# A two-layer hybrid trunk on one core: the layer passage reordered, one power of two a layer for the mix, and one product of the output norm as a square on ScalarE

## The chip, the cores and the metric

The kernel runs on one core of a Trainium2 chip. The metric is the device time of one execution in microseconds (us), lower is better. Before the change the median of three runs is 1673.27 us (1671.96 to 1673.34).

## The reference

Two layers, each with one pre-norm mixer. `h = rmsnorm(x) * g` goes through one input projection, whose columns feed three head groups: a gated short convolution, stick-breaking attention, and gated linear attention (GLA). Each branch is multiplied by a gate of its own, the three are concatenated and go through one output projection into the residual stream.

```python
D_MODEL, SEQ, DEPTH = 2048, 512, 2
def _layer(x, norm_g, w_in, ..., w_out):
    h = _rmsnorm(x, norm_g)
    proj = h @ w_in                                  # 2048 x 7184
    cv_h, cv_b, cv_c, cv_g, sb_q, sb_k, sb_v, sb_g, gl_q, gl_k, gl_v, gl_g, gl_lr = split(proj)
    y_conv = short_conv(cv_h, cv_b, cv_c, ...) * silu(cv_g)
    y_sb = stick_breaking(rmsnorm(sb_q), rmsnorm(sb_k), sb_v) * silu(sb_g)
    g = log_sigmoid(gl_lr @ gla_w_up + gla_b_up) / 16
    y_gla = rmsnorm(gla(gl_q, gl_k, gl_v, g), gla_on_g) * silu(gl_g)
    mix = concat([y_conv, y_sb, y_gla])
    return x + mix @ w_out
```

All of it is float32. Several of the gains drawn for the test are large, so the kernel scales operands by powers of two before it splits them.

## The kernel before

**Three-pass products.** TensorE (PE) multiplies float16. Each float32 operand is scaled by a power of two and split into a high and a low float16 part; a product is high*high + high*low + low*high. So every weight and every activation needs one pass on ScalarE (ACT) for the high part and one on VectorE (DVE) for the low part.

**Weight groups.** The weights stream from DRAM in groups of 256 columns, in a fixed list (`specs`): for GLA V, V with the low-rank columns, Q, K and two gate groups; then the convolution and the attention groups; then eight output groups, `gi` 0 to 7. A group passes through these steps, each for two halves of the rows: `fetch` (L332, a 1 MB DMA from SP's queue into an `st` buffer), `wmax` (L344, a sum of squares on ACT into `wm`), an all-reduce on GpSimd (POOL, L357, `wgm`), `wscale` (L360, L369, L371 on DVE: `wq`, `ws`, `wu`), and then four pieces `w` with the high part on ACT (L419) and the low part on DVE (L423). `st` buffers are reused: a fetch waits on SP until the low part of an earlier group has read its buffer.

**Order.** The code is written in program order and a scheduler orders each engine's instructions by a simulated timeline; `tc.high_priority()` lifts a piece. Engines work in order. So small edits of the code can move instructions on several engines.

**PSUM.** `cols(o)` multiplies one group into two PSUM banks of the pool `psp` (three banks), one per half of the 256 columns. The banks are free for the next group once they have been read for the last time. In GLA, q and k (`qT`, `kT`) are read twice from PSUM: the largest magnitude (L921 on DVE), then, after an all-reduce on POOL (L185, `qTgm`, `kTgm`) and `pow2` (L191 to L193, three small operations on DVE), the scaled copy (L930 on ACT). Behind K come the two gate groups, evicted by L816 to L823 (`gx` in the waits). GLA's source and target tiles (`th`) are zeroed by POOL (L907), as are the tiles `zw` and `raw` for column sums of x (L972).

**Mix.** The outputs of the branches get one common power of two. Each of eight pieces has a bound; `mixscale` turns each into a power of two by `pow2` and writes it to one column of `pmix`. `mix_unit` (L1079) all-reduces `pmix` on POOL, takes the largest and derives the factor.

**Output norm of GLA** (L1061 to L1075, eight times). The mean square `ms` is made by PE, `r` = exp(-0.5 ln(ms + eps)) on ACT, and one Newton step on DVE: (ms + eps) * r (L1070), * r (L1071), - 3, * r (L1072), * -0.5 * o (L1073).

**Layer passage.** Group `gi` 7 of layer 0 is multiplied block by block of 128 tokens, t = 0 to 3. `finish` adds the residual (L1359 on DVE, into the tile `x`, called `xt` in the code), stores it to DRAM (`xs<-x`, L1341, SP) and sums its squares (L1347, ACT). `xprep` then prepares the next layer's input for that block: `xnorm` (small operations, L490 to L494 on DVE, L198 and L199 on ACT), `xgain` (L499, two halves, in place in `x`), and the split. For t = 0 and 1 the split is made first (L536 ACT, L537 DVE, tiles `th` for the two halves of t = 0, `raw` and `qp` for those of t = 1) and each part is transposed by a DMA on SP's queue (L539). For t = 2 and 3 PE transposes (L509) into PSUM (`psz`, two banks), ACT takes the high part (L511) and DVE the low (L518), which frees the bank. The results are the tiles `act_183` (high) and `act_184` (low), from which the next layer's first group is multiplied (L649).

Of the kernel before, what the change touches and what calls it, by code (L numbers as in the profile page):

```python
# [10 lines left out]
AF = mybir.ActivationFunctionType  # L11
# [6 lines left out]
P = 128  # L18
# [21 lines left out]
def hybrid_trunk(ctx, tc, x, norm_g, w_in, conv_w, conv_b, sb_qn_g, sb_kn_g,  # L40
# [274 lines left out]
        with tc.high_priority():  # L315
            load_(i)

    staged, peak, scales = {}, {}, {}

    def junk(n):  # L320

# [18 lines left out]
    def wmax(i, h):  # L340

        if h == 0:
            peak[i] = sm(2 + len(specs[i][2]) // 2, "wm")
        S.activation(junk(HK * GW).rearrange("p (k n) -> p k n", k=HK), staged[i][h], AF.Square,  # L344
                     accum_out=peak[i][:, h:h + 1])
# [135 lines left out]

    ssq = sm(NT * NG, "ssq").rearrange("p (t g) -> p t g", g=NG)
    xscale = {}

    def xnorm(l, t):

# [9 lines left out]

    def xgain(t, h):
        xv = xt[t // 2][:, t % 2, h * (D // 2):(h + 1) * (D // 2)]
        V.scalar_tensor_tensor(xv, xv, xscale[t], gb[h], ALU.mult, ALU.mult)  # L499

    xps = {}

# [285 lines left out]
    for l in range(depth):  # L788
# [39 lines left out]

        pmix = sm(8, "pmix")

        def mixscale(j, m, tag):

            pow2(pmix[:, j:j + 1], m, -12.0, tag)

        def spill(k, y):

            nc.sync.dma_start(mixd[k], y)
# [78 lines left out]
        for tag in ("qT", "kT"):  # L916
            o = wk([P, 2, seq], tag)
            ps, u = cols(o)
            mx = sm(2, tag + "mx")
            for c in range(2):  # L920
                V.tensor_reduce(mx[:, c:c + 1], ps[c], AX.X, ALU.max, apply_absolute_value=True)  # L921
            gm = allmax(mx, 2, tag)
            m = sm(1, tag + "m")
            V.tensor_tensor(m, gm[:, 0:1], gm[:, 1:2], ALU.max)
            p2 = sm(1, tag + "p2")
            pow2(p2, m, -14.0, tag)
            s_ = sm(1, tag + "s")
            V.reciprocal(s_, p2)
            for c in range(2):
                S.activation(o[:, c, :], ps[c], AF.Copy, scale=s_)  # L930
# [9 lines left out]
        for p in range(2):  # L940
            gmx = sm(1, "ggm")
            gg.append(gate(gmx))
            m = sm(1, "gb")
            V.tensor_tensor(m, gmx, onmax[:, l:l + 1], ALU.mult)
            mixscale(6 + p, m, "g")

        def split_src(e, dst, b):

# [20 lines left out]
        for p in range(2):  # L969
# [88 lines left out]
            for hh in range(2):  # L1058
                ops_ = ops2[:, hh, :]

                o_ = wk([P, seq], "za")  # L1061
                S.activation(o_, ops_, AF.Copy, scale=gu[:, p:p + 1])
                sq = wk([P, seq], "e")
                S.activation(sq, o_, AF.Square)
                ms = bank(psm, "m")
                T.matmul(ms, avg.to_broadcast([P, P]), sq, start=True, stop=True)
                r_ = wk([P, seq], "e")
                S.activation(r_, ms, AF.Ln, bias=epst)
                S.activation(r_, r_, AF.Exp, scale=-0.5)
                V.scalar_tensor_tensor(sq, ms, EPS, r_, ALU.add, ALU.mult)  # L1070
                V.tensor_tensor(sq, sq, r_, ALU.mult)  # L1071
                V.scalar_tensor_tensor(r_, sq, 3.0, r_, ALU.subtract, ALU.mult)  # L1072
                V.scalar_tensor_tensor(r_, r_, -0.5, o_, ALU.mult, ALU.mult)  # L1073
                V.scalar_tensor_tensor(o_, r_, pcol("on", l), gg[p][:, hh, :], ALU.mult, ALU.mult)
                spill(12 + 2 * p + hh, o_)  # L1075

        def mix_unit():

            pmx = allmax(pmix, 8, "r")  # L1079
            V.tensor_reduce(pmx[:, 0:1], pmx, AX.X, ALU.max)  # L1080
            ratio[l] = sm(1, "rub")
            V.tensor_scalar(ratio[l], pmx[:, 0:1].bitcast(I32), 1.0, (51 - 127 - MAGIC) * 2.0 ** 23, ALU.mult, ALU.add)
            rp = sm(1, "rpm")
            V.reciprocal(rp, pmx[:, 0:1])
            return rp
# [62 lines left out]
        def conv_out(j, y, then=lambda: None):  # L1148

            g = gate()  # L1150
            V.tensor_tensor(y, y, g, ALU.mult)
            bound = sm(2, "cm")

            def limit(m):
                V.tensor_reduce(m, y, AX.XY, ALU.max, apply_absolute_value=True)
                return m

            then()
            s_ = None
            if j:  # L1160
                V.tensor_scalar(bound[:, 1:2], limit(bound[:, 0:1]), loaded[cursor[0]][1], 2.0 ** 28, ALU.mult, ALU.mult)
                mixscale(j, bound[:, 1:2], "c")
                s_ = mix_unit()
            ps, u = cols(None if j else wk([P, 2, seq], "qT"))
            for c in range(2):
                V.scalar_tensor_tensor(m32[0][:, 2 + c, :] if j else y[:, c, :], ps[c], u, y[:, c, :], ALU.mult, ALU.mult)
            if not j:
                mixscale(j, limit(bound[:, 0:1]), "c")
                for c in range(2):
                    spill(2 * j + c, y[:, c, :])  # L1170
            return s_
# [94 lines left out]
        for j in range(4):  # L1266
# [40 lines left out]
            if j:  # L1307
                vh, vl, vu = value_group()
            g = gate(bm[:, 1:2])
            m = sm(1, "sbm")  # L1310
            V.tensor_scalar(m, bm[:, 1:2], vu, 2.0 ** 28, ALU.mult, ALU.mult)
            mixscale(2 + j, m, "b")
            attend(j, *qkT, vh, vl, vu, g)
            go()

# [22 lines left out]
        def land(gi, dst, t, n, c0, w, ot):  # L1338

            to = out[0] if last else xs  # L1340
            nc.sync.dma_start(to[t * P:(t + n) * P, c0:c0 + w].rearrange("(t p) c -> p t c", p=P), dst)  # L1341
            if not last:
                if ot is not None:
                    nc.sync.dma_start(xt[t // 2][:, t % 2:t % 2 + n, c0:c0 + w], dst)

        def square(gi, t, dst):
# [107 lines left out]
```

## Time and profile before

| | |
|---|---|
| Median of three runs | 1673.27 us |
| The profiled execution | 1674.31 us, of it a span of 1672.2 us |
| TensorE clock granted | 0.998 |
| PE busy | 1640.1 us of 17450 matmuls, 98% |
| DVE busy | 1420.5 us, 85% |
| ACT busy | 1233.2 us, 74% |
| POOL busy | 74.0 us, 4% |

"Busy" counts instructions that do work; an engine's waits are its idle time. PE is nearly always busy, so a change can save at most the waits of PE, unless it changes the products themselves, which this one does not.

### The profile page before, as it was taken

To read this page: it belongs to the slowest core of one execution; us is meant where nothing else is said; L and a number is where in the kernel's file an instruction comes from. 1 tells how busy PE (TensorE), PEld (TensorE's weight loads), DVE (VectorE), ACT (ScalarE), POOL (GpSimd) and SP (SyncE) were. 2 spreads that over 40 slices of the span, in tenths; PEclk is the share of its full clock that TensorE was granted. 3 is DMA by queue.
4 is the path that set the end of the run, shared out by engine and by line. 5 is a ranking of instruction groups with operands and counts; after the bars stand their busy time and mean duration, and the time that the engine had idled before them with its cause. 6 is when DMAs were issued, how large, how long until landed. Compare 5 with 4: busy or idle time off the path is not lost.

```text
span 1672.2 us, 40635 instructions
## 1 busy us (share of the span) xinstructions
PE 1640.1 (98%) x17450; PEld 1331.6 (80%) x17450; DVE 1420.5 (85%) x2368; ACT 1233.2 (74%) x1695; POOL 74.0 (4%) x96
## 2 busy tenths in 40 slices
PE   7999999999999999999999999999999999999999
PEld 5744748999999985799976447589989998858999
DVE  7967898899898987888778588988989899979896
ACT  8767776697878787667766678776969696976663
POOL 0010000000000000000000100000000000000000
PEclk9999999999999999999999999999999999999999
DMA  7393332436363649245765624324464546473441
GB/s 259 104 206 94 102 107 68 130 85 169 101 161 112 159 126 259 78 158 161 226 140 143 159 76 121 107 82 109 118 155 118 155 116 158 123 237 102 153 153 52
DMA packets 308099, 227.58 MB, mean 136 GB/s; under 512 B 127650, under 2 KB 301004, under 8 KB 307408
## 3 DMA queue, kind: packets, MB, share of 16 engines
q1 hardware_dynamic: 298912, 215.55, 46.4%
q10 hardware_dynamic: 9008, 9.45, 1.8%
q8 instruction: 136, 2.23, 0.6%
q14 instruction: 43, 0.35, 0.1%
HBM read 179.88 MB, written 14.68 MB: 116 GB/s over the span
## 4 chain that ended last, share of the span: by engine, by line
issue 30%; PE 13%; DVE 5%; ACT 4%; DMA 2%; POOL 1%; SPq 0%; POOLq 0%; DVEq 0%; ACTq 0%
PE psp L676 3%; PE psp L649 2%; PE psp L673 2%; PE psp L623 2%; PE psp L622 2%; PE psp L621 2%; POOL wgm L357 1%; DVE w L437 1%; ACT w L436 1%; ACT junk L344 1%; DMA st<-in_w_in_dram 1%; DVE w L423 1%; PE psp L639 0%; PE psp L638 0%; PE psp L637 0%
## 5 line engine op out<-in xcount | busy, mean ns | idle before, releaser
L436 ACT ACTIVATE w<-st,ws 128x1024 f16<-128x1024 f32 x273 | 305.2, 1141 | 137.7 <-DVE st L441 63.7
L437 DVE SCALAR_TENSOR_TENSOR w<-st,ws,w 128x1024 f16<-128x1024 f32 x273 | 344.5, 1279 | 61.3 <-ACT w L436 58.4
L344 ACT ACTIVATE junk<-st 128x2048 uint8<-128x2048 f32 x150 | 284.9, 1899 | 22.3 <-DMA st<-in_w_in_dram 16.0
L673 PEld LDWEIGHTS <-w 128*128 128x128 f16 x2352 | 230.2, 98 | 32.2 <-DVE u L716 2.3
L637 PE MATMUL psp<-w,act 128*128 128x256 f16 x896 | 244.1, 273 | 0.0
L638 PE MATMUL psp<-w,act 128*128 128x256 f16 x896 | 244.1, 273 | 0.0
L639 PE MATMUL psp<-w,act 128*128 128x256 f16 x896 | 243.9, 273 | 0.0
L676 PE MATMUL psp<-w,act 128*128 128x128 f16 x3600 | 214.7, 219 | 5.9 <-DVE raw L727 2.5
L621 PE MATMUL psp<-act,w 128*128 128x512 f16 x576 | 218.3, 379 | 2.0 <-DVE gx L823 1.3
L622 PE MATMUL psp<-act,w 128*128 128x512 f16 x576 | 218.3, 379 | 0.0
L623 PE MATMUL psp<-act,w 128*128 128x512 f16 x576 | 218.1, 379 | 0.0
L676 PEld LDWEIGHTS <-act 128*128 128x128 f16 x3600 | 205.0, 98 | 9.6 <-issue 5.1
L423 DVE SCALAR_TENSOR_TENSOR w<-st,ws,w 128x1024 f16<-128x1024 f32 x148 | 187.9, 1278 | 28.5 <-ACT w L419 28.1
L419 ACT ACTIVATE w<-st,ws 128x1024 f16<-128x1024 f32 x144 | 161.9, 1140 | 32.5 <-PE psp L623 22.5
L676 PE MATMUL psp<-w,s 128*128 128x128 f16 x2688 | 156.3, 219 | 0.5 <-DVE vv L719 0.5
L673 PE MATMUL psp<-s,w 128*128 128x256 f16 x1344 | 156.6, 274 | 0.0
L676 PEld LDWEIGHTS <-s 128*128 128x128 f16 x2688 | 152.1, 98 | 2.1 <-issue 1.9
L357 POOL PARTITION_ALL_REDUCE wgm<-wm x75 | 57.8, 770 | 1444.3 <-ACT junk L344 1343.2
L673 PE MATMUL psp<-act,w 128*128 128x256 f16 x1008 | 118.3, 273 | 0.0
L649 PE MATMUL psp<-w,act 128*128 128x256 f16 (+1 forms) x960 | 111.7, 277 | 6.0 <-DMA act<-raw 2.6
L649 PEld LDWEIGHTS <-act 128*128 128x128 f16 x960 | 93.8, 99 | 22.0 <-issue 2.9
L622 PEld LDWEIGHTS <-w 128*128 128x128 f16 x576 | 56.3, 98 | 67.6 <-issue 2.5
(361 smaller groups left out, 2652.4 us busy)
## 6 DMA issues: line engine op xcount, KB each, us to landing
st<-in_w_in_dram SPq DMA_DIRECT2D x120, 1024.0 KB, 5.8
st<-in_w_out_dram SPq DMA_DIRECT2D x32, 1024.0 KB, 5.7
m<-mixd SPq DMA_DIRECT2D x24, 256.0 KB, 5.4
x<-in_x_dram SPq DMA_DIRECT2D x4, 1024.0 KB, 11.9
qT<-in_x_dram ACTq DMA_DIRECT2D x8, 512.0 KB
qT<-xs ACTq DMA_DIRECT2D x8, 512.0 KB, 3.8
out_dram<-kT SPq DMA_DIRECT2D x16, 256.0 KB, 2.1
mixd<-e SPq DMA_DIRECT2D x12, 256.0 KB
```

Of the source, the lines that this page charges most:

```text
L344: S.activation(junk(HK * GW).rearrange("p (k n) -> p k n", k=HK), staged[i][h], AF.Square, accum_out=peak[i][:, h:h + 1])
L436: his.setdefault(i, []).append(S.activation(hi, x, AF.Copy, scale=scales[i]))
L437: V.scalar_tensor_tensor(lo, x, scales[i], hi, ALU.mult, ALU.subtract)
L621: T.matmul(o, wh, xh[:, k, :, :], start=st_, stop=False)
L622: T.matmul(o, wh, xl[:, k, :, :], start=False, stop=False)
L623: T.matmul(o, wl, xh[:, k, :, :], start=False, stop=en)
L637: T.matmul(o, xh[:, k, t, :], wh, start=k == 0 and t % 2 == 0, stop=False, skip_group_check=True)
L638: T.matmul(o, xh[:, k, t, :], wl, start=False, stop=False, skip_group_check=True)
L639: T.matmul(o, xl[:, k, t, :], wh, start=False, stop=k == lastk, skip_group_check=True)
L649: T.matmul(o[:, :n], a_[:, k, t, :], wview(w, part, k, n), start=i == 0 and k == 0, stop=i == 2 and k == KT - 1)
L673: T.matmul(o[:, :2 * P], ww, x[xi][:, k, :, :], start=first, stop=final, skip_group_check=True)
L676: T.matmul(o[:, t * P:(t + 1) * P], x[xi][:, k, t, :], ww, start=first, stop=final, skip_group_check=True)
```

## The change

1. **Mix.** `mixscale` is gone: the raw bounds go into `pmix`, and one `pow2` is applied to their maximum in `mix_unit`.
2. **Output norm.** The two DVE products (ms + eps) * r * r become a square of r on ACT and one DVE product with it.
3. **GLA q and k.** Both banks are copied to SBUF on ACT at once (the new L923); the maximum and the scaled copy (now L926 and L935) read and write that copy.
4. **Passage.** The result of `gi` 7 goes to a tile `ot` (tag `kT`) of its own, kept in `tail`, and is stored from there; `xgain`'s second half is made in two pieces, 768 columns in place and 256 columns from `ot`. The squares of the second half of `gi` 6 (t = 2 and 3) are issued behind the squares of the next weight group (`issue_after`).

```diff
-        S.activation(junk(HK * GW)..., staged[i][h], AF.Square, accum_out=peak[i][:, h:h + 1])
+        squares[i] = S.activation(junk(HK * GW)..., staged[i][h], AF.Square, accum_out=peak[i][:, h:h + 1])
...
     def xgain(t, h):
         xv = xt[t // 2][:, t % 2, h * (D // 2):(h + 1) * (D // 2)]
-        V.scalar_tensor_tensor(xv, xv, xscale[t], gb[h], ALU.mult, ALU.mult)
+        n = D // 2 - (GW if h and tail else 0)
+        V.scalar_tensor_tensor(xv[:, :n], xv[:, :n], xscale[t], gb[h][:, :n], ALU.mult, ALU.mult)
+        if h and tail:
+            V.scalar_tensor_tensor(xv[:, n:], tail[0][:, t, :], xscale[t], gb[h][:, n:], ALU.mult, ALU.mult)
...
-        def mixscale(j, m, tag):
-            pow2(pmix[:, j:j + 1], m, -12.0, tag)
...
             for c in range(2):
+                if ps[c].tensor is not o.tensor:
+                    with tc.high_priority():
+                        S.activation(o[:, c, :], ps[c], AF.Copy)
+            ps = [o[:, c, :] for c in range(2)]
+            for c in range(2):
                 V.tensor_reduce(mx[:, c:c + 1], ps[c], AX.X, ALU.max, apply_absolute_value=True)
...
-            m = sm(1, "gb")
-            V.tensor_tensor(m, gmx, onmax[:, l:l + 1], ALU.mult)
-            mixscale(6 + p, m, "g")
+            V.tensor_tensor(pmix[:, 6 + p:7 + p], gmx, onmax[:, l:l + 1], ALU.mult)
...
-                V.scalar_tensor_tensor(sq, ms, EPS, r_, ALU.add, ALU.mult)
-                V.tensor_tensor(sq, sq, r_, ALU.mult)
+                S.activation(sq, r_, AF.Square)
+                V.scalar_tensor_tensor(sq, ms, EPS, sq, ALU.add, ALU.mult)
...
             V.tensor_reduce(pmx[:, 0:1], pmx, AX.X, ALU.max)
+            pow2(pmx[:, 0:1], pmx[:, 0:1], -12.0, "r")
...
-                if ot is not None:
+                if ot is not None and gi < 2:
                     nc.sync.dma_start(xt[t // 2][:, t % 2:t % 2 + n, c0:c0 + w], dst)
...
-            ot = wk([P, NT, GW], "kT") if last or gi < 2 else None
+            ot = wk([P, NT, GW], "kT") if last or gi < 2 or gi == NG - 1 else None
+            if gi == NG - 1:
+                tail.append(ot)
...
+                        if gi == NG - 2 and r:
+                            late = dst
+                            continue
...
                 for t, o, u in project_by_token(GW):
+                    if not (last or t):
+                        with tc.issue_after(squares[cursor[0]].ins):
+                            for i in range(2):
+                                square(gi - 1, 2 + i, late[:, i, :])
```

(The convolution's and the attention's calls of `mixscale` are replaced in the same way.)

The scheduler moves instructions in three places that matter below. Lines behind L344 are one to four higher after the change, so L423 stays L423 while L499 becomes L501 and L503, L537 becomes L541, and L1359 becomes L1360.

The first place is the passage. On DVE, before, the rows from the residual of t = 0 (`psp_12016`) to the first `xgain`; `w_12004` and `w_12007` are the first low parts of the next weight group:

```order
L1359 SCALAR_TENSOR_TENSOR x_9456<-psp_12016,wu_11605,qT_11983 128x256
L360 TENSOR_SCALAR wq_11996<-wgm_11997 128x1
L490 TENSOR_REDUCE xtot_12069<-ssq_9458 128x1
L369 TENSOR_SCALAR ws_12000<-wq_11996 128x1
L371 TENSOR_SCALAR wu_12002<-wq_11996,xub 128x1
L201 TENSOR_SCALAR xrm_12075<-xtot_12069 128x1
L850 TENSOR_SCALAR gu_12359<-wu_12002 128x1
L423 SCALAR_TENSOR_TENSOR w_12004<-st_11590,ws_12000,w_12004 128x1024
L1359 SCALAR_TENSOR_TENSOR x_9456<-psp_12095,wu_11605,qT_11983 128x256
L423 SCALAR_TENSOR_TENSOR w_12007<-st_11590,ws_12000,w_12007 128x1024
```

After, on the same engine, the same stretch (`w_11971` and `w_11974` are those low parts now):

```order
L360 TENSOR_SCALAR wq_11963<-wgm_11964 128x1
L369 TENSOR_SCALAR ws_11967<-wq_11963 128x1
L371 TENSOR_SCALAR wu_11969<-wq_11963,xub 128x1
L850 TENSOR_SCALAR gu_12334<-wu_11969 128x1
L423 SCALAR_TENSOR_TENSOR w_11971<-st_11560,ws_11967,w_11971 128x1024
L423 SCALAR_TENSOR_TENSOR w_11974<-st_11560,ws_11967,w_11974 128x1024
L1360 SCALAR_TENSOR_TENSOR kT_11951<-psp_11983,wu_11575,qT_11949 128x256
```

The scale of the next group and two of its low parts now stand ahead of the residual of t = 0. Further on, around the fourth residual (`psp_12265`, after the change `psp_12239`), DVE's order is, before and then after:

```order
L1359 SCALAR_TENSOR_TENSOR x_9457<-psp_12265,wu_11605,qT_11983 128x256
L423 SCALAR_TENSOR_TENSOR w_12013<-st_11592,ws_12000,w_12013 128x1024
L537 TENSOR_TENSOR raw_12163<-x_9456,raw_12163 128x1024
L204 TENSOR_TENSOR xrt_12235<-xrt_12235,xrm_12233 128x1
L537 TENSOR_TENSOR qp_12169<-x_9456,qp_12169 128x1024
```

```order
L541 TENSOR_TENSOR raw_12135<-x_9426,raw_12135 128x1024
L204 TENSOR_TENSOR xrt_12208<-xrt_12208,xrm_12206 128x1
L423 SCALAR_TENSOR_TENSOR w_11977<-st_11562,ws_11967,w_11977 128x1024
L1360 SCALAR_TENSOR_TENSOR kT_11951<-psp_12239,wu_11575,qT_11949 128x256
L205 SCALAR_TENSOR_TENSOR xrstd_12202<-xrt_12208,xr_1205_12203 128x1
L541 TENSOR_TENSOR qp_12142<-x_9426,qp_12142 128x1024
```

The low part of `raw` no longer stands behind two weight parts. At the end of the passage, before, one low part of t = 2 (L518) stands ahead of `xgain` of t = 3; after, both (L522) stand behind it and behind four weight pieces:

```order
L518 TENSOR_TENSOR act_184<-psz_12242,act_183 128x8x128
L857 TENSOR_SCALAR gu_12359<-wu_12378 128x1
L499 SCALAR_TENSOR_TENSOR x_9457<-x_9457,xrs_12330,g_9459 128x1024
L499 SCALAR_TENSOR_TENSOR x_9457<-x_9457,xrs_12330,g_9460 128x1024
L425 SCALAR_TENSOR_TENSOR w_12380<-ga_11989,ws_12376,w_12380 128x4x16
```

```order
L503 SCALAR_TENSOR_TENSOR x_9427<-kT_11951,xrs_12304,g_9430 128x256
L857 TENSOR_SCALAR gu_12334<-wu_12353 128x1
L425 SCALAR_TENSOR_TENSOR w_12355<-ga_11956,ws_12351,w_12355 128x4x16
L423 SCALAR_TENSOR_TENSOR w_12355<-st_11952,ws_12351,w_12355 128x4x256
L425 SCALAR_TENSOR_TENSOR w_12360<-ga_11956,ws_12351,w_12360 128x4x16
L423 SCALAR_TENSOR_TENSOR w_12360<-st_11952,ws_12351,w_12360 128x4x256
L522 TENSOR_TENSOR act_184<-psz_12215,act_183 128x8x128
L522 TENSOR_TENSOR act_184<-psz_12228,act_183 128x8x128
```

So the banks of t = 2 are freed later in the row than before. On SP's queue the transposes of t = 1 stand after the change as

```order
L543 DMA_TRANSPOSE act_183<-raw_12135 128x8x128
L543 DMA_TRANSPOSE act_184<-raw_12135 128x8x128
L543 DMA_TRANSPOSE act_183<-qp_12142 128x8x128
L1342 DMA xs<-kT_11951 128x256
L543 DMA_TRANSPOSE act_184<-qp_12142 128x8x128
L332 DMA st_12337<-in_w_in_dram 128x8x256
```

where before a weight fetch and a store stood between the second transpose (`qp`, high) and the third (`raw`, low); the fetch now stands behind all of them.

The second place is GLA's k in layer 1, on ACT. Before, the copies of `kT` stand behind the two squares of a weight group:

```order
L344 ACTIVATE junk_13408,wm_13407<-st_13252 128x2048
L344 ACTIVATE junk_13410,wm_13407<-st_13254 128x2048
L930 ACTIVATE kT_13101<-psp_13131,kTs_13241 128x512
L930 ACTIVATE kT_13101<-psp_13132,kTs_13241 128x512
L950 ACTIVATE th_12946<-e_13554 128x4x64
```

After, the banks are read ahead of them:

```order
L923 ACTIVATE kT_13078<-psp_13108 128x512
L419 ACTIVATE w_13248<-st_13079,ws_13244 128x1024
L923 ACTIVATE kT_13078<-psp_13109 128x512
L419 ACTIVATE w_13251<-st_13079,ws_13244 128x1024
L344 ACTIVATE junk_13382,wm_13381<-st_13231 128x2048
L344 ACTIVATE junk_13384,wm_13381<-st_13233 128x2048
L935 ACTIVATE kT_13078<-kT_13078,kTs_13220 128x512 x2
```

The third place is POOL in layer 0, before and after:

```order
L185 ISA qTgm_1165<-qTmx_1162 128x2
L972 MEMSET zw_1631 128x1024
L357 ISA wgm_1341<-wm_1335 128x2
L972 MEMSET raw_1978 128x1024
L185 ISA kTgm_1311<-kTmx_1308 128x2
```

```order
L975 MEMSET zw_1625 128x1024
L185 ISA qTgm_1167<-qTmx_1162 128x2
L357 ISA wgm_1345<-wm_1339 128x2
L975 MEMSET raw_1972 128x1024
L185 ISA kTgm_1315<-kTmx_1310 128x2
```

The zeroing of `zw` moved ahead of the all-reduce for q's maximum.

More of the change, by code (lines that the diff above doesn't have):

```diff
@@ L316, in load @@
             load_(i)
-    staged, peak, scales = {}, {}, {}
+    staged, peak, scales, squares = {}, {}, {}, {}
     def junk(n):
@@ L343, in wmax @@
             peak[i] = sm(2 + len(specs[i][2]) // 2, "wm")
-        S.activation(junk(HK * GW).rearrange("p (k n) -> p k n", k=HK), staged[i][h], AF.Square,
-                     accum_out=peak[i][:, h:h + 1])
+        squares[i] = S.activation(junk(HK * GW).rearrange("p (k n) -> p k n", k=HK), staged[i][h], AF.Square,
+                                  accum_out=peak[i][:, h:h + 1])
         if h and len(specs[i][2]) > 1:
@@ L483, in hybrid_trunk @@
     xscale = {}
+    tail = []
     def xnorm(l, t):
@@ L1151, in conv_out @@
             V.tensor_tensor(y, y, g, ALU.mult)
-            bound = sm(2, "cm")
+            bound = sm(1, "cm")
             def limit(m):
@@ L1160, in conv_out @@
             if j:
-                V.tensor_scalar(bound[:, 1:2], limit(bound[:, 0:1]), loaded[cursor[0]][1], 2.0 ** 28, ALU.mult, ALU.mult)
-                mixscale(j, bound[:, 1:2], "c")
+                V.tensor_scalar(pmix[:, j:j + 1], limit(bound), loaded[cursor[0]][1], 2.0 ** 28, ALU.mult, ALU.mult)
                 s_ = mix_unit()
@@ L1167, in conv_out @@
             if not j:
-                mixscale(j, limit(bound[:, 0:1]), "c")
+                limit(pmix[:, j:j + 1])
                 for c in range(2):
@@ L1309, in hybrid_trunk @@
             g = gate(bm[:, 1:2])
-            m = sm(1, "sbm")
-            V.tensor_scalar(m, bm[:, 1:2], vu, 2.0 ** 28, ALU.mult, ALU.mult)
-            mixscale(2 + j, m, "b")
+            V.tensor_scalar(pmix[:, 2 + j:3 + j], bm[:, 1:2], vu, 2.0 ** 28, ALU.mult, ALU.mult)
             attend(j, *qkT, vh, vl, vu, g)
```

## The prediction

> **What bounds the kernel now.** I read the page first. Its first rows give the share of each engine:
>
> ```profile
> span 1672.2 us, 40635 instructions
> PE 1640.1 (98%) x17450; PEld 1331.6 (80%) x17450; DVE 1420.5 (85%) x2368; ACT 1233.2 (74%) x1695; POOL 74.0 (4%) x96
> ```
>
> PE is idle for 1672.2 - 1640.1 = 32.1 us. The products stay as they are, so the whole gain must come out of these 32.1 us, and what DVE or ACT save elsewhere is worth nothing unless PE waits for it. The waits of PE by releaser (sum in us, times, longest) say where such places are; the first word pair is the waiting line, the second what it waited for:
>
> ```profile
> PE psp L676 <- DVE w L437: 3.5, 4, 1.1
> PE psp L649 <- DMA act<-raw: 2.6, 1, 2.6
> PE psp L676 <- DVE raw L727: 2.5, 3, 0.9
> PE psp L621 <- DVE gx L823: 1.3, 1, 1.3
> PE psp L649 <- DMA act<-th: 0.9, 2, 0.6
> PE psp L621 <- ACT kT L930: 0.7, 1, 0.7
> ```
>
> Three of the edits touch such rows. The two of L649 are the layer passage: 2.6 + 0.9 = 3.5 us. The two of L621 are GLA's banks: 0.7 us in layer 0, 1.3 us in layer 1. Together 5.5 us of 1672, 0.33%, is what the change can take away directly. PE's timeline shows the passage (start, duration, form, idle time before it in brackets):
>
> ```profile
> 849.88 1.93 PE L649 MATMUL psp<-w,act 128*128 128x256 f16 x16 [0.63 <-DMA act<-th]
> 852.11 5.71 PE L649 MATMUL psp<-w,act 128*128 128x256 f16 x48 [0.30 <-DMA act<-th]
> 857.66 2.06 PE L509 MATMUL psz<-ident,x 128*128 128x128 f32 x16
> 862.32 4.54 PE L649 MATMUL psp<-w,act 128*128 128x256 f16 x40 [2.60 <-DMA act<-raw]
> 866.70 1.04 PE L509 MATMUL psz<-ident,x 128*128 128x128 f32 x8
> ```
>
> PE waits twice for block t = 0 and once, the longest, for the low part of t = 1.
>
> **The passage, part 4.** What makes t = 0 late is the row of DVE, and ahead of that of ACT:
>
> ```profile
> 831.52 0.42 ACT L1347 ACTIVATE junk<-x 128x256 uint8<-128x256 f32 x1 [3.74 <-DVE x L1401]
> 832.65 1.91 ACT L344 ACTIVATE junk<-st 128x2048 uint8<-128x2048 f32 x1
> ```
>
> ```profile
> 834.88 0.48 DVE L1359 SCALAR_TENSOR_TENSOR x<-psp,wu,qT 128x256 f32<-128x256 f32 x1 [3.45 <-PE psp L649]
> 837.23 0.21 DVE L360 TENSOR_SCALAR wq<-wgm 128x1 f32<-128x1 int32 x1 [1.86 <-POOL wgm L357]
> 840.11 0.48 DVE L1359 SCALAR_TENSOR_TENSOR x<-psp,wu,qT 128x256 f32<-128x256 f32 x1
> 840.51 1.28 DVE L423 SCALAR_TENSOR_TENSOR w<-st,ws,w 128x1024 f16<-128x1024 f32 x1
> 842.61 2.48 DVE L499 SCALAR_TENSOR_TENSOR x<-x,xrs,g 128x1024 f32<-128x1024 f32 x2
> ```
>
> ACT idles 3.74 us for a residual of gi 6 (L1401), squares it (two squares, 831.52 to 832.65) and only then comes to the weight squares. Put behind them, the squares of gi 6 give the weight scale up to 3.74 + 1.13 = 4.9 us back; I take 4.2, as the load of ACT just before may take some. The scale (837.23) comes at 833.0, and two low parts of 1.28 us are done by about 836.8, ahead of the second residual. The residual of t = 0, which now stands behind them, goes from 834.88 to 836.8; its norm has until 840.6, so that costs nothing. `xgain` of t = 0 can start when the second residual ends, 840.11 + 0.48 = 840.6 instead of 842.61: 2.0 us earlier. Its third piece costs about 0.2 us (256 columns as in the residual's 0.48, less the 0.32 that the shortened piece saves). So the transposes of t = 0 come 1.8 us earlier, and the waits of 0.63 and 0.30 go. For t = 1:
>
> ```profile
> 853.32 1.22 DVE L537 TENSOR_TENSOR raw<-x,raw 128x1024 f16<-128x1024 f32 x1
> 859.79 1.23 DVE L518 TENSOR_TENSOR act<-psz,act 128x1024 f16<-128x1024 f32 x1
> 861.00 2.47 DVE L499 SCALAR_TENSOR_TENSOR x<-x,xrs,g 128x1024 f32<-128x1024 f32 x2
> 863.58 1.28 DVE L423 SCALAR_TENSOR_TENSOR w<-st,ws,w 128x1024 f16<-128x1024 f32 x1
> ```
>
> ```profile
> 854.81 0.53 SPq L332 DMA_DIRECT2D st<-in_w_in_dram  x1
> 856.14 2.20 SPq L539 DMA_TRANSPOSE act<-raw  x1
> ```
>
> The low part of `raw` (853.32) loses two weight parts and a residual ahead of it (2 x 1.28 + 0.48 = 3.0) and follows an `xgain` that starts about 0.7 us earlier (the residual of t = 2, which PE sets, holds it): about 849.6. On SP's queue its transpose no longer stands behind a 1 MB fetch (854.81). It was issued at 856.14 and released PE at 862.32, 6.2 us later. Of the transposes of `qp` the DMA table says (us from issue to landing, last):
>
> ```profile
> act<-qp SPq DMA_TRANSPOSE x2, 3.2
> ```
>
> Issued at about 851 it lands between 854.2 and 857.2 by these two rows; without a fetch ahead I take 3.2. PE comes to it at about 856 (857.66, less the 0.93 of waits gone, and six of these products now stand ahead of the transposes of t = 2), so this wait, 2.60, goes too, or up to 1.2 of it stays.
>
> The Trainium skill says in "DMA: Bandwidth & Descriptors", section "Queues, rings and completion order", that each of the 16 DMA engines takes a queue's descriptors in ring order; by that rule the transpose behind the fetch pays for most of its megabyte, and moving the fetch takes the wait away, the sum as above. If instead a transpose took 6.2 us by itself, 1.2 us would stay. The 6.2 us behind a fetch against 3.2 agrees with the rule, though the two were not issued at the same load.
>
> What is late next are the low parts of t = 2. Before, one is made at 859.79, ahead of `xgain` of t = 3. Now both stand behind that `xgain` (2.5 us) and two weight parts with their small companions (3.0 us), and PE's first transposes of t = 3 need the bank that they free, at 866.70 - 3.5 = 863.2 if the other waits are gone. With `xgain` of t = 3 starting at 858.5, which follows from moving the row by the 2.5 us that DVE is ahead, the first low part ends at 858.5 + 2.5 + 3.0 + 1.2 = 865.2: a wait of 2.0. If it starts 2 us earlier, none. I take 1.2 of new wait. Passage: 3.5 - 1.2 = 2.3 gained, ends 1.0 and 3.5.
>
> The fetch's other side: `st` for the second half of a later group is now issued behind the last transposes, about 3 us later than 854.81. What hides it is the stock of weights ahead of PE, which was busy without a gap from 870 to 960 (window, length, busy time of PE, PEld, DVE, ACT, POOL, clock, DMA share, GB/s):
>
> ```profile
> 870.00:960.00 90.00, 90.00 (x548) 53.26 (x547) 57.99 (x102) 54.94 (x73) 10.75 (x10) 1.00 0.60 144
> ```
>
> So I cost it at nothing; if that cover were gone it would cost up to these 3 us.
>
> **GLA q and k, part 3.** Layer 1, first ACT, then POOL, then PE:
>
> ```profile
> 949.30 1.91 ACT L344 ACTIVATE junk<-st 128x2048 uint8<-128x2048 f32 x1 [3.66 <-DMA st<-in_w_in_dram]
> 951.20 1.25 ACT L930 ACTIVATE kT<-psp,kTs 128x512 f32<-128x512 f32 x2
> 959.80 1.73 ACT L959 ACTIVATE th<-e 64x256 f16<-64x256 f32 x4 [6.03 <-POOL th L907]
> 965.33 0.67 ACT L816 ACTIVATE ga<-psp,nu 128x512 f32<-128x512 f32 x1
> ```
>
> ```profile
> 957.97 1.80 POOL L907 MEMSET th<- 128x2048 f16 x1 [4.57 <-issue]
> ```
>
> ```profile
> 969.74 0.38 PE L621 MATMUL psp<-act,w 128*128 128x512 f16 x1 [1.29 <-DVE gx L823]
> ```
>
> The gate's bank is read at 965.33 because ACT had waited for a fetch (3.66) and then for a memset (6.03). With k's banks read before, and the fetch taken out from behind transposes, ACT is 3 to 4 us earlier there, against a wait of 1.29: gained 1.2, ends 0 and 1.29. The eight new copies, 0.63 us each by L930's 1.25 for two (5.0 us), lie beside PE's products of the same groups; ACT is busy for 74%. In layer 0 the wait of 0.68 goes, but POOL's order changes:
>
> ```profile
> 93.40 0.40 POOL L185 PARTITION_ALL_REDUCE qTgm<-qTmx  x1 [6.48 <-DVE qTmx L921]
> 99.68 0.95 POOL L972 MEMSET zw<- 128x1024 f32 x1 [5.88 <-DMA s<-zw]
> ```
>
> The memset waits for a DMA until 99.68, and the all-reduce of q now waits behind it: 100.6 instead of 93.4, 7.2 us. Behind it on ACT stand q's scaled copies and GLA's decays, so its chain runs some 5 us later, and the gate banks with it. No row of layer 0 prices that. The nearest is layer 1, whose POOL has this order already: a wait of 1.29. Between 0 and 1.29 I take 0.5. Layer 0: -0.68 + 0.5 = -0.2, ends -0.7 and +0.6.
>
> **The small operations, parts 1 and 2.** Their prices (count, min/median/max ns, first and last start):
>
> ```profile
> L193 DVE TENSOR_SCALAR pmix<-bpc x8: 141/144/155, 366.8 to 1446.7; 128x1 f32<-128x1 f32 x8
> L1071 DVE TENSOR_TENSOR e<-e,e x8: 682/689/693, 209.8 to 1131.2; 128x512 f32<-128x512 f32 x8
> L1064 ACT ACTIVATE e<-za x8: 613/627/630, 203.4 to 1120.2; 128x512 f32<-128x512 f32 x8
> ```
>
> Sixteen times three operations become two times three: 42 x 0.145 = 6.1 us less on DVE. In the chain to the common factor nothing is saved: three operations that stood ahead of the all-reduce stand behind it. Eight products leave DVE, 5.5 us, and eight squares come to ACT, 5.0 us. Where PE waits for DVE (w L437 3.5, raw L727 2.5) the rows are mostly of attention and of output groups, where little of this is. I take 0.3 us of gain; ends 1.0 of gain (a sixth of those 6 us) and 0.5 of loss, should ACT's extra 10.0 us delay high parts of weights.
>
> **Sum.** 2.3 + 1.2 + 0.2 + 0.3 = 4.0 us off the profiled execution's 1674.31, which gives 1670.3. That execution lies 1.0 us over the median of the runs; against the median, 1673.27 - 4.0 = 1669.3.
>
> **Rivals.**
> *The passage gives it back* (0.30). The low parts of t = 2 keep PE for the full 2.0 us, and 1.2 of the low part of t = 1 stays: 3.5 - 3.2 = 0.3 of the passage, total 0.3 + 1.7 = 2.0, 1671.3. For it speaks DVE's busy time in the stretch; against it that the weight parts may have slid forward too.
> *Layer 0 eats it* (0.10). The late chain of q costs 1.29 at two gate banks, 2.6 in all, and layer 1 keeps its 1.29: 4.0 - 2.1 - 1.2 = 0.7, 1672.6. Against it: k's and q's banks are free early.
> *The order of the weights becomes the wait* (0.08, the other side). The residual of t = 0 stands behind two low parts, and these behind the scale. Had the scale no gain (837.23), that residual came at 841.8, and, with some 3 us for its norm (square, root, small operations), `xgain` at 845.3: 2.7 us later than 842.61, and with it all that follows; the total is 2.7 - 1.7 = +1.0, 1674.3. It is slower by more than 0.2%, 1676.6, from a scale at 839.6 on. Against it: ACT idles 3.74 us there, and the fetch of that group had long been issued:
>
> ```profile
> 818.92 2.77 SPq L332 DMA_DIRECT2D st<-in_w_in_dram  x2
> ```
>
> *The parts with no PE wait behind them* are no rival: they give nothing either way.
>
> **Numbers.** The forecast's own case has 0.52, from 1667.0 to 1670.5. All terms at their good ends give 3.5 + 1.3 + 0.7 + 1.0 = 6.5, 1666.8; the first two rivals reach to 1672.6, the third beyond. So the range is 1666.6 to 1672.8. A difference of 0.2%, 3.35 us, is about what can be told from no change: the bounds are 1669.9 and 1676.6. Of the forecast's case some four fifths lie below 1669.9 (0.42), and of the first rival a quarter, where its 2.0 us of wait shrinks (0.07): faster 0.49. Of the third rival some six tenths lie above 1676.6: slower 0.05. The remaining 0.46 is no change.
>
> **What would show it.** Right: no idle time of PE at `act<-th` and `act<-raw`, the first weight scale of the passage near 833, `xgain` of t = 0 near 840.6; no wait for kT in layer 0 or for `gx` in layer 1. Right on the rest: a new wait of PE's t = 3 transposes for L522 of 0 to 2 us. Wrong: a wait for that of over 2 us, `act<-raw` still late although no fetch stands ahead of it, waits for gate banks in layer 0 from 120 to 145 of over 1.3, or new waits in attention, where I expect none.

## The result, and the profile after

The changed kernel takes 1669.68 us (median of 12 runs, 1666.79 to 1671.14) against 1672.78 us before (12 runs, 1670.39 to 1675.82). The ratio is 0.9983, 95% interval 0.9975 to 0.9990: 3.1 us or 0.17% less, where the prediction had 4.0 us. That is a change of less than 0.2%, though the interval leaves out a ratio of 1. The page of the profiled execution:

```profile
span 1668.4 us, 40601 instructions
PE 1641.0 (98%) x17450; PEld 1332.4 (80%) x17450; DVE 1413.9 (85%) x2322; ACT 1242.0 (74%) x1711; POOL 72.8 (4%) x96
```

DVE has 6.6 us less work, ACT 8.8 more, and PE's idle time fell from 32.1 to 27.4 us. The waits of PE (sum, times, longest):

```profile
PE psp L653 <- ACT act L515: 1.6, 2, 1.4
PE psp L653 <- DMA act<-raw: 1.4, 1, 1.4
PE psp L625 <- DVE gx L827: 0.9, 1, 0.9
```

The rows of `act<-th` and of `kT` are gone, as forecast. `act<-raw` is not, `act L515` is new, and the row of `gx` belongs to layer 0 now. PE in the passage, in order of time:

```profile
835.76 14.79 PE L653 MATMUL psp<-w,act 128*128 128x256 f16 x134
851.97 6.51 PE L653 MATMUL psp<-w,act 128*128 128x256 f16 x58 [1.42 <-DMA act<-raw]
858.31 1.91 PE L513 MATMUL psz<-ident,x 128*128 128x128 f32 x16
860.06 3.00 PE L653 MATMUL psp<-w,act 128*128 128x256 f16 x26
864.42 1.95 PE L653 MATMUL psp<-w,act 128*128 128x256 f16 x16 [1.35 <-ACT act L515]
866.21 1.04 PE L513 MATMUL psz<-ident,x 128*128 128x128 f32 x8
```

Two waits, 2.8 us, stand where three stood, 3.5 us. DVE, then ACT, then SP's queue in the same stretch:

```profile
832.43 0.21 DVE L360 TENSOR_SCALAR wq<-wgm 128x1 f32<-128x1 int32 x1 [1.00 <-POOL wgm L357]
836.51 0.47 DVE L1360 SCALAR_TENSOR_TENSOR kT<-psp,wu,qT 128x256 f32<-128x256 f32 x1
839.43 2.20 DVE L501 SCALAR_TENSOR_TENSOR x<-x,xrs,g 128x1024 f32<-128x1024 f32 x2
848.19 1.22 DVE L541 TENSOR_TENSOR raw<-x,raw 128x1024 f16<-128x1024 f32 x1
864.39 2.35 DVE L522 TENSOR_TENSOR act<-psz,act 128x1024 f16<-128x1024 f32 x2
```

```profile
846.85 1.06 ACT L540 ACTIVATE raw<-x 128x1024 f16<-128x1024 f32 x1 [0.66 <-DVE x L501]
861.47 1.89 ACT L344 ACTIVATE junk<-st 128x2048 uint8<-128x2048 f32 x1
863.36 1.91 ACT L515 ACTIVATE act<-psz 128x1024 f16<-128x1024 f32 x2
```

```profile
841.82 6.17 SPq L543 DMA_TRANSPOSE act<-th  x4
848.71 2.62 SPq L543 DMA_TRANSPOSE act<-raw  x2
```

The scale of the next weight group comes at 832.43 instead of 837.23 and `xgain` of t = 0 at 839.43 instead of 842.61, so the parts of t = 0 land in time. PE stops at 850.55, for the high part of `raw`, the first of t = 1. That part was made by 847.9, its transpose was issued at 848.71 behind four of t = 0, and PE goes on with it at 851.97. PE was not through with t = 0 when it stopped. Its own order, in the built program, has changed, which the section on the change did not say: before, all 48 products of t = 0 stand ahead of the first product of t = 1; after, only 12 do, then come eight with the high part of `raw`, and the other 36 of t = 0 stand behind these. The low parts of t = 0 landed at 848.67 and 849.85 (the landings in the trace), ahead of the stop. The second wait is for the high parts of t = 2, which stand on ACT behind a weight square (861.47).

**Stage by stage.** The same product (the n-th matmul of a line; inside a stage the order can differ, so only the ends are used) can be found in two profiles. The difference of its start is PE's lead (negative: ahead of the profile before), and how the lead changes between the ends of a stage is what the stage gained or lost. The table has this for all the kernels run, in us; times are those of the profile before.

| kernel | GLA banks, layer 0 (113-229) | norm, layer 0 (229-303) | 534-767 | passage (842-900) | gates, layer 1 (900-1058) | norm, layer 1 (1058-1132) |
|---|---|---|---|---|---|---|
| the changed one | +0.13 | +0.43 | -0.39 | -1.36 | -1.53 | +0.42 |
| p_only | -0.53 | -0.01 | -2.27 | -1.23 | -1.14 | -0.03 |
| q_only | -0.40 | 0.00 | -2.74 | +1.02 | -1.34 | -0.02 |
| m_only | -0.63 | -0.02 | -1.89 | -0.04 | -0.46 | -0.03 |
| n_only | -0.38 | +0.38 | -2.50 | +0.10 | -0.52 | +0.37 |
| no_n | -0.36 | 0.00 | -2.01 | -1.49 | -1.54 | -0.02 |
| a_hi | +0.44 | +0.40 | -0.19 | -2.17 | -1.47 | +0.42 |
| b_v1 | -0.42 | +0.02 | -3.79 | -0.11 | -0.54 | -0.01 |
| best_v1 | -0.19 | 0.00 | -3.45 | -2.15 | -1.10 | -0.02 |
| a_pool | -0.92 | +0.40 | -2.40 | -1.02 | -1.54 | +0.42 |
| best2 | -0.93 | +0.01 | -3.50 | -2.11 | -1.25 | -0.04 |

A stage that an edit doesn't touch shows the scatter between executions: nothing in the norm stages (0.05), 0.4 to 0.5 in the GLA stage of layer 0 (p_only, n_only, b_v1), 0.5 in the gates (n_only, b_v1), and 2 in the stretch from 534 to 767, of which the last section tells. All leads are against one profile of the kernel before, which was slow in these stages.

### The profile page after: what moved, and what is told of

Same layout as the page of the kernel before. It is cut to its first block, busy times and chain, and to the rows that moved or that the text cites. A ratio compares the mean times of both kernels' runs of the same rounds, so it can differ in the third digit from the quotient of the medians.

```text
span 1668.4 us, 40601 instructions
## 1 busy us (share of the span) xinstructions
PE 1641.0 (98%) x17450; PEld 1332.4 (80%) x17450; DVE 1413.9 (85%) x2322; ACT 1242.0 (74%) x1711; POOL 72.8 (4%) x96
## 4 chain that ended last, share of the span: by engine, by line
PE 25%; DVE 11%; issue 10%; ACT 6%; DMA 2%; POOL 1%; SPq 1%; ACTq 0%; POOLq 0%; DVEq 0%
PE psp L680 5%; PE psp L677 5%; PE psp L653 3%; DVE w L437 3%; ACT w L436 2%; PE psp L627 2%; PE psp L625 2%; PE psp L626 2%; PE psp L642 1%; PE psp L643 1%; PE psp L641 1%; ACT junk L344 1%; DMA st<-in_w_in_dram 1%; DVE th L963 1%; DVE w L423 1%
## 5 line engine op out<-in xcount | busy, mean ns | idle before, releaser
L344 ACT ACTIVATE junk<-st 128x2048 uint8<-128x2048 f32 x150 | 284.9, 1899 | 14.8 <-DMA st<-in_w_out_dram 6.8
L677 PEld LDWEIGHTS <-w 128*128 128x128 f16 x2352 | 230.2, 98 | 32.1 <-DVE u L720 2.1
L423 DVE SCALAR_TENSOR_TENSOR w<-st,ws,w 128x1024 f16<-128x1024 f32 x148 | 187.5, 1279 | 26.5 <-ACT w L419 26.1
```

What stands on the lines that cost most here:

```text
L344: squares[i] = S.activation(junk(HK * GW).rearrange("p (k n) -> p k n", k=HK), staged[i][h], AF.Square, accum_out=peak[i][:, h:h + 1])
L677: T.matmul(o[:, :2 * P], ww, x[xi][:, k, :, :], start=first, stop=final, skip_group_check=True)
```

## The experiments

**The parts alone.** Each is the kernel before with one part of the diff. p_only is part 4 (`squares`, `tail`, `xgain` in pieces, `issue_after`), q_only part 3, m_only part 1, n_only part 2. Their core lines:

```diff
p_only  +            ot = wk([P, NT, GW], "kT") if last or gi < 2 or gi == NG - 1 else None
p_only  +                        with tc.issue_after(squares[cursor[0]].ins):
q_only  +                        S.activation(o[:, c, :], ps[c], AF.Copy)
m_only  +            pow2(pmx[:, 0:1], pmx[:, 0:1], -12.0, "r")
n_only  +                S.activation(sq, r_, AF.Square)
n_only  +                V.scalar_tensor_tensor(sq, ms, EPS, sq, ALU.add, ALU.mult)
```

> Part 4 alone (the layer passage) on the kernel before. Theory: the parts act at separate places and add up; the passage alone brings the 1.4 us that PE is ahead of before from 872 us on in the profile after, so 1671.4 to 1672 against 1672.8, with waits of about 1.4 us for the low part of t = 1 and 1.35 us for the high part of t = 2, and no shift of PE anywhere else. Rival: the passage only pays with the other parts, or its gain is eaten in layer 1: no difference.

Measured: 1669.03 us against 1671.62, ratio 0.9988 (0.9979 to 0.9997). PE gains 1.23 us in the passage, with the same two waits as in the changed kernel:

```profile
848.25 6.50 PE L653 MATMUL psp<-w,act 128*128 128x256 f16 x58 [1.55 <-DMA act<-raw]
860.70 1.95 PE L653 MATMUL psp<-w,act 128*128 128x256 f16 x16 [1.36 <-ACT act L515]
```

The passage is the one part of the change whose gain alone is clear in the times. Against the theory, PE also gains 1.14 us at layer 1's gates, where only this is left of the wait of 1.29 (sum, times, longest; 0.16 to two digits):

```profile
PE psp L625 <- DVE gx L827: 0.2, 1, 0.2
```

> Part 3 alone (q and k copied out of PSUM). Theory: the gate banks' wait of layer 1 goes (1.3 to 1.4 us), in layer 0 the wait for kT (0.7) goes and one of about 0.9 for the gate bank comes: 1.2 us less in all, and POOL's order of layer 0 with zw ahead of q's all-reduce comes from this part. Rival: the gain in layer 1 came from the passage or from the mix, then this part alone keeps the 1.29 and is even or slower.

Measured: 1671.56 us, ratio 0.9997 (0.9988 to 1.0006). The wait at layer 1's gates is gone (-1.34). POOL's order of layer 0 comes with this part, and with it a wait for the gate bank. But kernels without this part also gain there, as the wait of 1.29 in the profile before was the longest of all that I saw. Without parts 3 and 4 the gate stage leads by 0.38 us on average (the kernel before at 0, m_only, n_only and b_v1 at 0.46 to 0.54); with part 4 alone by 1.14, with part 3 alone by 1.34, and with both by 1.41 (six kernels). So the rival is half right: both parts take the same wait away. Part 3 is worth some 1.0 us without part 4 and some 0.3 beside it, each read from a single profile of the one part alone. In layer 0 the five kernels with the part and the new POOL order average -0.08, those without it -0.39: a loss of 0.3. The balance, some 0.7 us for the part alone, is below what these times can tell.

> Part 1 alone (one power of two for the mix). Theory: the 2.2 us by which PE gains in the attention stretches of both layers (290 to 755 and 1120 to 1430 us) come from the 42 small operations that left DVE ahead of operands that PE waits for: 1 to 2 us less, all of it there. Rival: they come from the output norm's product that left DVE, or are differences of DMA timing between executions: then this part changes nothing (within 0.5 us).

Measured: 1671.83 us, ratio 0.9999 (0.9990 to 1.0008): nothing. The theory falls. The gains in attention are scatter: from 1132 to 1513 us the lead changes by -0.86 here, but also by -1.01 in b_v1 and -0.61 in n_only, which keep the sixteen powers of two, and by +0.55 in a_hi, which does not.

> Part 2 alone (the square on ScalarE). Theory: it costs 0.4 us in each layer, 0.8 in all: new waits of PE for the GLA operands th, which ACT makes and which now stand behind squares, at about 267 and 1094 us. Rival: these waits come from the late q chain of part 3, and this part alone gains up to 1 us or nothing.

Measured: 1671.43 us, ratio 1.0005 (0.9996 to 1.0014). The times don't decide, but the stages do: every kernel with the square loses 0.37 to 0.43 us in each norm stage, and none without it loses over 0.02. PE's waits for the GLA operands, before and then n_only:

```profile
266.90 1.36 PE L965 MATMUL psz<-th,th 128*128 128x256 f16 x11 [0.43 <-DVE th L960]
```

```profile
266.65 0.27 PE L965 MATMUL psz<-th,th 128*128 128x256 f16 x1 [0.23 <-ACT th L959]
268.35 0.38 PE L965 MATMUL psz<-th,th 128*128 128x256 f16 x2 [0.23 <-DVE th L960]
```

PE waits twice, once for ACT, where it waited once. A product behind a wait starts later by more than the bracket says (0.39 for 0.23, 0.60 for 0.43, by the usual interval of 0.11 between these products), since the end of the one ahead is modelled. Two of 0.39 against one of 0.60 make 0.2 us. The other 0.2 stands in two later products of L965, which start 0.16 and 0.05 late without a bracket (273.96 and 275.52).

**The square undone in the changed kernel.**

```diff
-                S.activation(sq, r_, AF.Square)
-                V.scalar_tensor_tensor(sq, ms, EPS, sq, ALU.add, ALU.mult)
+                V.scalar_tensor_tensor(sq, ms, EPS, r_, ALU.add, ALU.mult)
+                V.tensor_tensor(sq, sq, r_, ALU.mult)
```

> The changed kernel with part 2 undone (the product of the output norm back on VectorE). Theory from the run of part 2 alone: the square costs 0.4 to 0.5 us in each layer, so this is 0.9 us under the changed kernel, 0.20 to 0.25% under the kernel before; PE's waits for the operands th near 267 and 1094 us are back to one of 0.43. Rival: the waits belong to the late chain of q and stay: no difference to the changed kernel (0.17%).

Measured: 1669.11 us against 1671.43, ratio 0.9982 (0.9973 to 0.9990). Both norm stages are back at 0.00 and -0.02, so the square is the cause. The ratio is that of the changed kernel within its interval: a difference of 0.8 us can't be seen in these times.

**The weight square behind the high parts of t = 2.**

```diff
-        S.activation(dst[0][:, h * HK:(h + 1) * HK, t, :], ps, AF.Copy)
+        xhi[t, h] = S.activation(dst[0][:, h * HK:(h + 1) * HK, t, :], ps, AF.Copy)
...
+        third = i == [p[0] for p in specs].index(1) + 2 and h == 0
+        with tc.issue_after(xhi[2, 1].ins) if third else contextlib.nullcontext():
             squares[i] = S.activation(junk(HK * GW)..., staged[i][h], AF.Square, ...)
```

> The changed kernel, with one weight square (the first half of the third weight group of layer 1, L344) issued behind the high parts of t = 2. Theory: the 1.35 us that PE waits for the high part of t = 2 come from that square ahead of it on ScalarE; without it PE waits some 0.6 us for the bank that the low part of t = 2 frees: 0.7 us gained in the passage. Rival, the prediction's own step: VectorE's low part is what counts, the wait only changes its name and stays over 1 us.

Measured: 1668.35 us, ratio 0.9980 (0.9972 to 0.9989). PE:

```profile
859.43 4.75 PE L656 MATMUL psp<-w,act 128*128 128x256 f16 x42
864.90 1.09 PE L516 MATMUL psz<-ident,x 128*128 128x128 f32 x8 [0.72 <-DVE act L525]
```

The wait for ACT is gone, and the next one is DVE's low part at 0.72, as expected; the passage gains 2.17 us where the changed kernel has 1.36.

**A product that waits, put behind others.** One of PE's longest waits of the kernel before lies outside the change, in attention:

```profile
629.08 0.37 PE L1235 MATMUL psm<-th,v 128*128 128x256 f16 x1 [2.21 <-DMA th<-za]
```

```diff
                 for n, (qtiles, cols) in enumerate(CHUNKS):
+                    for _ in range(1 if l == 0 and j == 3 and hh == 0 and n else 0):
+                        T.matmul(op[:, 0:2, :]..., vh[:, 0, hs], nil, start=False, stop=False, ...)
```

(`nil` is a column of zeros, broadcast, so that the product adds nothing.)

> The kernel before with one useless product (of zeros, added to the same bank) ahead of the second chunk's products of the fourth attention pair of layer 0. The scheduler then puts the product that waits 2.21 us at 629 behind 94 others, so that this wait goes. Theory of the clock: a wait of 2 us in one window of 3.41 us also halves the next window's clock, which costs 1.7 us more whenever it happens (two of six profiles here): PE gains 2.2 us in the stretch from 534 to 767 us against profiles without a halved window there, 4 us against those with one, and the kernel 2.2 us and up to 1 more, 0.13 to 0.19%. Rival: the wait comes back behind another product, or the clock costs nothing: 0 to 2.2 us, 0 to 0.13%.

Measured: 1668.49 us against 1671.43, ratio 0.9981 (0.9972 to 0.9990): as much as the whole change. The lead from 534 to 767 us grows by 3.79, against 0.2 to 0.4 in the profiles with a halved clock there and 1.89 to 2.74 in those without; most of the difference between the two groups is the clock's share, as the last section works out.

**POOL's order of layer 0 restored.** `reduced["qT"]` is the all-reduce of q's maximum. (The memset of the tag `zw` clears GLA's tile of scores, which shares the tag with the column sums of x; it waits for their transposes. The section on the kernel before said it otherwise.)

```diff
-            G.memset(attd, 0.0)
+            with tc.issue_after(reduced["qT"].ins):
+                G.memset(attd, 0.0)
```

> The changed kernel, with POOL's memset of GLA's tile (tag zw) issued behind the all-reduce of q's maximum, as the kernel before had it in layer 0, and in layer 1 too. Theory (the prediction's step for layer 0): the wait for the gate bank near 140 us, 0.3 to 1.2 us in the five profiles with part 3, comes from the late chain of q; it goes, PE gains 0.4 to 0.9 us between 113 and 157 us, the time goes to 0.20 to 0.23% under the kernel before. Rival: the wait comes from the later kT, or from another queue; then it stays.

Measured: 1668.00 us against 1671.55, ratio 0.9979 (0.9970 to 0.9988). POOL in the changed kernel, and here:

```profile
99.85 0.95 POOL L975 MEMSET zw<- 128x1024 f32 x1 [12.25 <-DMA s<-zw]
100.78 0.40 POOL L185 PARTITION_ALL_REDUCE qTgm<-qTmx  x1
```

```profile
94.69 0.40 POOL L187 PARTITION_ALL_REDUCE qTgm<-qTmx  x1 [7.08 <-DVE qTmx L928]
99.91 0.95 POOL L978 MEMSET zw<- 128x1024 f32 x1 [4.83 <-DMA s<-zw]
```

The all-reduce comes 6 us earlier. The gate bank's wait, in the changed kernel

```profile
141.09 0.38 PE L625 MATMUL psp<-act,w 128*128 128x512 f16 x1 [0.89 <-DVE gx L827]
```

is gone, and the stage gains 0.92 where that kernel loses 0.13. The late chain of q was the cause. a_pool and best2, with part 3 and the old order, lead by 0.92 and 0.93 in this stage; without the part it is 0.39, and with the part and the new order 0.08. So the part's own gain in layer 0 is some 0.5 us, and the new order costs some 0.85.

**Together.** best_v1 has parts 1, 3 and 4, the square of weights behind the high parts, and the useless product; best2 has POOL's order too.

> Parts 1, 3 and 4 of the change without part 2, with the weight square behind the high parts of t = 2 and with the useless product: if all parts add up, 0.17% + 0.05% + 0.04% + 0.15%, 0.4% under the kernel before, 1665 us where that has 1671.6. Rival: they share the same slack, and it stays at 0.25%.

Measured: 1665.59 us, ratio 0.9960 (0.9947 to 0.9972). The parts add up, and the rival's 0.25% lies outside the interval.

> The best version so far (parts 1, 3 and 4, the weight square behind the high parts, the useless product), with the same order on POOL. Theory: 0.3 to 0.6 us under the 0.40% of that version, 1665.0 where the kernel before has 1671.5. Rival: no difference, 0.40%.

Measured: 1665.11 us against 1671.55, ratio 0.9964 (0.9952 to 0.9977). Its stage in layer 0 gains 0.7 us over best_v1's (-0.93 against -0.19); the two times can't be told apart, and the rival stands as far as they go. Both beat the kernel before and the changed one.

## Why the prediction was nearly right

**The sum** was 4.0 us for 3.1 measured, and the nearness is in part luck. By the stages all four terms came out lower than forecast: 1.4 us for 2.3, 1.0 for 1.2, a loss of 0.3 for a gain of 0.2, and a loss of 0.8 for a gain of 0.3. That makes 1.3 us, less than the lower end of what was measured (1.7 to 4.2 by the interval).

The lists of the runs show a gain that the sum did not have. The mean granted clock is 0.99936 over the 56 runs of the five kernels that have part 4 without the useless product (changed, p_only, no_n, a_hi, a_pool) and 0.99889 over 108 runs of the kernel before, q_only, m_only and n_only. The difference, 0.0005 (standard error 0.0001) of some 1670 us, is about 0.8 us: half a window of halved clock, as the last section explains, less in each run. Part 4 shortens the waits of the passage, and in q_only, which lacks it, such a window fell just there. That it is the passage's windows that are fewer is argued, not shown, as the place of a window is known for the profiled executions alone.

**The passage, 2.3 forecast, 1.4 measured (1.02 to 1.49 in four kernels).** Its first steps held: the scale at 833.0 (832.43), the residual of t = 0 at 836.8 (836.51), `raw`'s low part at about 849.6 (848.19), and no wait for t = 0. `xgain` came at 839.43, not 840.6: I took the second residual for bound by PE, but it had stood behind a weight part on DVE. The step that failed is "this wait, 2.60, goes too", and with it came a sign that I had listed for being wrong, `act<-raw` late although no fetch stands ahead. I followed the low part of `raw` alone, and that one is in time: it landed at 853.40, and PE read it at 857.66. But I took PE's order as it was, and in the new one eight products with the high part stand ahead of 36 of t = 0. PE came to them 1.4 us before that part had landed, with work of t = 0 ready behind them. Twelve of the 36 had their operands, the low parts and three weight pieces; at 0.109 us each that is 1.3 us, nearly the whole wait. This is an estimate: no run put them ahead. p_only has the same order and the same wait, to 848.25, with the low parts of t = 0 landed at 844.84 and 846.02.

The step on t = 2 had the right place, and its price, 1.2 us for 1.35, came out by luck, as the engine was the wrong one. PE's next products read the high part, which ACT ended at about 864.4 behind a weight square; the transposes that need the bank freed by DVE come after them. a_hi shows DVE's own wait behind it, at 0.72.

The transposes' landing agrees with what I took: issued at 848.71 without a fetch ahead, `raw`'s high part released PE 3.3 us later, against 6.2 behind a fetch. The Trainium skill's ring order ("DMA: Bandwidth & Descriptors", "Queues, rings and completion order") is in line with that; no run here varied the fetch alone.

**Layer 1's gates, 1.2 forecast, about 1.0 measured** for parts 3 and 4 together (1.41 against 0.38). Part 3 does what was forecast: with it ACT reads k's banks early, and in q_only the wait is gone. The other cause that I gave, the fetch out of the way of the transposes, is not seen: in p_only ACT still waits 3.20 us for the fetch, against 2.98 to 3.66 without either part, though PE's wait for the gates falls to 0.16. Why part 4 alone does that stays open. The size was read from one execution, whose 1.29 was the longest of the waits seen without these parts (0.75 to 1.29).

**Layer 0, a gain of 0.2 forecast, a loss of 0.3 measured**, with the mechanism shown by a_pool: the memset ahead of q's all-reduce, the late chain, a gate bank late by 0.89, in a range of 0 to 1.29 of which I took 0.5. The wait for `kT` that was to pay for it was 0.68 in one execution and 0.14 to 0.31 in the others.

**The small operations, 0.3 forecast.** The powers of two gave nothing that can be measured, though 6 us of DVE work went: PE did not wait for them. The square cost 0.8 us, more than the 0.5 I set as the worst end. I looked for its price where DVE is awaited, but it is ACT that makes half of GLA's operands.

**The rivals.** "The passage gives it back" came half true, by another way: the 1.4 us lie midway between its 0.3 and the forecast's 2.3. "Layer 0 eats it" came in its mechanism, at a third of its price. The order of the weights did not become the wait.

## What to carry to other kernels

When a wait is removed, look first whether the waiting engine's own order is still the same, and then ask for each operand of its next product when it arrives. Here the wait went over to the other half of a split operand, whose products had moved ahead of work that was ready. A term read from one execution's wait of a microsecond may be off by that much: stage by stage leads over several kernels, with the untouched stages as a measure of the scatter, resolve 0.4 us where the times resolve 1.5. Work that leaves a busy engine is worth what its successor waits for, and work that goes to a half-idle one can still be late there.

## What the runs showed of the hardware

A wait of PE can cost more than its length. The profile before has a stretch behind the wait of 2.21 us in which PE's granted clock was half (window, length, busy time of PE, PEld, DVE, ACT and POOL with counts, granted clock, DMA share, GB/s); a_hi, with a wait of 2.27, has it too, and m_only, with 1.92, not:

```profile
629.00:632.00 3.00, 2.92 (x14) 2.02 (x14) 3.00 (x4) 1.70 (x3) 0.00 (x0) 0.51 1.01 337
```

```profile
629.00:632.00 3.00, 3.00 (x15) 2.07 (x15) 3.00 (x4) 1.17 (x2) 0.00 (x0) 0.50 1.08 335
```

```profile
629.00:632.00 3.00, 3.00 (x30) 2.69 (x29) 3.00 (x5) 1.73 (x4) 0.00 (x0) 1.00 1.07 341
```

14 and 15 products against 30 in the same 3 us. The half clock lasted 3.41 us each time. In q_only it fell into the passage, and that kernel lost 1.02 us there. Its wait of PE (sum, times, longest; 1.95 us to two digits), and the stretch behind it:

```profile
PE psp L649 <- DMA act<-raw: 1.9, 1, 1.9
```

```profile
860.10:863.50 3.40, 3.40 (x19) 2.43 (x17) 3.40 (x6) 2.97 (x4) 0.00 (x0) 0.51 0.03 5
```

Away from the start and the end, it was there in four of the twelve profiles (before, changed, a_hi and q_only), behind waits of 1.95 to 2.27 us. The length of a wait alone does not decide it: the waits for `act<-raw` of 2.60 in the profile before and of 2.36 to 2.70 in m_only, n_only and b_v1 had a full clock behind them. In the profiles the changes of the granted clock lie on a grid of 3.413 us. On that grid each of these four waits falls into two windows, with at most 1.41 to 1.61 us in one. The four that were followed by a half clock put 1.95 to 2.16 us into one window, and the next window was the halved one. From 30 to 1660 us of all twelve profiles, every window in which PE idled 1.95 us or more was followed by a halved one, and none with 1.92 us or less was. From 534 to 767 us the three kernels with it lead by 0, 0.39 and 0.19, the six others with that wait (1.39 to 1.92 us) by 1.89 to 2.74, 2.1 us more on average, of which the shorter waits explain 0.5. So one such window costs an estimated 1.6 us, near the half of its 3.41. It also goes with part of the scatter: the 75 runs of the kernel before that were taken beside these experiments average 1671.0 us at a mean granted clock of 1.000, 1671.7 at 0.999, 1672.2 at 0.998 and 1674.1 at 0.997.

The Trainium skill ("TensorE: Matmul & The Clock Gate", "Part 1: The HAM clock gate") has the free-running window of 3413 ns and the half clock, and the traces agree with both. Its section "HAM oscillation — how this bites in real kernels" warns of idle gaps over some 3.4 us. Here the half clock followed waits of about 2 us, so the measurement differs from that bound.
